# Second layer's down projection: seven block products (Strassen's scheme) for each pair of column slices, in seven of eight row slices

## The chip, the cores and the metric

The kernel runs on one core of one Trainium2 chip. The metric is the device time of one execution in microseconds (us), measured over several runs; the median counts. A profile of one execution stands beside it. Engines: TensorE (PE, with its weight loads PEld), VectorE (DVE), ScalarE (ACT), GpSimd (POOL), and SyncE (SP), which issues most of the transfers.

## The reference, cut to what matters

A trunk of two layers over 256 tokens of 2048 features, in float32; each layer is a token mixer and then a squared-ReLU MLP with 8192 hidden features:

```
def mlp(h, w_up, w_down):
    a = jax.nn.relu(h @ w_up)          # (256 x 2048) @ (2048 x 8192)
    return (a * a) @ w_down            # (256 x 8192) @ (8192 x 2048)

for i in range(2):
    ...
    h = rms_norm(x, mlp_norm[i])
    x = x + mlp(h, mlp_w_up[i], mlp_w_down[i])
return rms_norm(x, final_norm)
```

## The kernel before, in words

All weights stream from HBM once. The whole program is a list of steps; each step brings one weight tile `raw` of 1 MB (128 partitions, 2048 numbers each), and is worked off in two halves of 128x1024. `split` (L110) turns a half into two parts: `hi`, the number rounded to the TensorE's float32r format (ACT, L118), and `lo`, the rest `raw - hi` (L125, on DVE, or on POOL for steps listed in `pool_lo`). The activations are split in the same way. A product of float32 numbers is then three matmuls: hi x hi, lo x hi, hi x lo. `run_steps` (L159) keeps loads three steps ahead and splits three halves ahead of the half that PE consumes; `raw` has 3 buffers, `hi` and `lo` 4 halves each. Order and overlap on the engines are settled when the program is built, by a scheduler that places instructions by their dependences and priorities; the order on each engine is fixed after that.

`mlp` (from L685) cuts the 8192 hidden features into eight slices of 1024. `up(s)` computes slice s in four quarters q of 256 features, two steps each (kc = 0, 1); a half takes 8 matmuls of 512 columns (`mm_f`, L199) and 8 of 256 (L202), and at the end of a quarter `relu2` (L804) adds the two parts (DVE L808, one input in PSUM), applies max and the token scale (DVE L810), squares (ACT L812) and splits the result into `rT`. `down(s)` multiplies a slice's activations by 1024 rows of `w_down`, in four column slices n of 512 with two steps each. A half takes 12 matmuls of 512 columns (`mm_t`, L222 to L224): 2 row blocks of 128, 2 token blocks of 128, 3 each. After each n, DVE adds the accumulator to `x` (L820). The order is up(0), up(1), down(0), up(2), down(1), ..., up(7), down(6), down(7). The second layer's part begins at about 1270 us; the last slice, down(7), runs beside the final norm.

Of the kernel before, what the change touches and what calls it, by code (L numbers as in the profile page):

```python
# [2 lines left out]

# [15 lines left out]
P = 128  # L19
EPS = 1e-6  # L20
D = 2048
T = 256
# [11 lines left out]
URGENT = 300  # L34


class Trunk:
    def __init__(self, ctx, tc, a, out):
        self.tc, self.nc, self.a = tc, tc.nc, a
        self.out = out[0].rearrange("(b p) c -> p b c", p=P)  # L40
        self.DF = a["mlp_w_up"].shape[2]
        pool = lambda name, bufs, **k: ctx.enter_context(tc.tile_pool(name=name, bufs=bufs, **k))
        self.const = pool("const", 1)
        self.w = pool("w", 3)
        self.blk = pool("blk", 6)
# [4 lines left out]
        self.dram = pool("dram", 1, space=DRAM)  # L50
        self.steps = []
        self.pending = []
        self.bg = []
        self.rate = self.credit = 0
        self.raws, self.parts = {}, {}
# [8 lines left out]
        return self.blk.tile(shape, dt, tag="blk", name=name)  # L64

    def t4(self, shape, name="t4"):
        return self.tmp.tile(shape, F32, tag="t4", name=name)

    def t2(self, shape, name="t2"):
        return self.tmp.tile(shape, F32, tag="t2", name=name, bufs=3)  # L70
# [9 lines left out]
    def add(self, view, shape, consume, pre=None):  # L80
        self.steps.append((view, shape, consume, pre))

    def add_f(self, w2d, k0, c0, consume, pre=None):
        self.add(w2d[k0 * P:(k0 + 8) * P, c0:c0 + 256].rearrange("(k p) n -> p k n", p=P), [P, 8, 256], consume, pre)

# [6 lines left out]
            self.fetched = self.nc.sync.dma_start(out=out, in_=in_)  # L92

    def load(self, i, half=None):
        view, shape, _, _ = self.steps[i]
        for kind in self.before_load.pop(i, ()):
            self.table(*kind)
        if not half:
            self.raws[i] = self.w.tile(shape, F32, tag="raw", name="raw", bufs=3)
        raw = self.raws[i]  # L100
        nk = shape[1] // 2
        k = slice(0, shape[1]) if half is None else slice(half * nk, half * nk + nk)
        if len(shape) == 4:
            for j in range(shape[2]):
                self.fetch(raw[:, k, j, :], view[:, k, j, :])
        else:
            self.fetch(raw[:, k], view[:, k])
        self.loaded = i + 1

    def split(self, h, urgent=True):  # L110
        i, half = divmod(h, 2)
        raw = self.raws[i] if half == 0 else self.raws.pop(i)
        nk = raw.shape[1] // 2
        sl = raw[:, half * nk:(half + 1) * nk]
        hi = self.w.tile([P, nk] + list(raw.shape[2:]), F32R, tag="hi", name="hi", bufs=4)
        lo = self.w.tile([P, nk] + list(raw.shape[2:]), F32R, tag="lo", name="lo", bufs=4)
        with self.tc.high_priority(offset=URGENT if urgent else 0):
            self.nc.scalar.activation(hi, sl, AF.Copy)  # L118
            eng = self.nc.gpsimd if i in self.pool_lo else self.nc.vector
            if self.barrier is not None and h == 2 * self.barrier + 2:  # L120
                self.low_late = lambda: eng.tensor_tensor(out=lo, in0=sl, in1=hi.bitcast(F32), op=ALU.subtract)
                self.parts[h] = (hi, lo)
                return None
            with self.behind(self.lo_gate) if self.lo_gate is not None else nullcontext():
                ins = eng.tensor_tensor(out=lo, in0=sl, in1=hi.bitcast(F32), op=ALU.subtract)  # L125
# [33 lines left out]
    def run_steps(self):  # L159
        n = 2 * len(self.steps)  # L160
        ns = 0
        for h in range(n):
# [7 lines left out]
            while self.loaded < min(len(self.steps), i + 4):  # L170
# [4 lines left out]
            if half == 0 and pre is not None:  # L175
                pre()
            hi, lo = self.parts.pop(h)
# [233 lines left out]
    def conv_in(self):  # L411
# [28 lines left out]

    def gate(self, c, A):
        nc = self.nc
        b_in = self.vec("b_in")
        t = self.tmp.tile([P, T], F32, tag="ga", name="ga", bufs=2)
        with self.tc.high_priority(offset=URGENT):
            nc.vector.tensor_tensor(out=A, in0=A, in1=self.rstdB.broadcast_to([P, 2, T]), op=ALU.mult)
# [238 lines left out]
    def mlp(self, layer, last_slice, last_block, hooks=None):  # L685
        w_up, w_dn = self.a["mlp_w_up"][layer], self.a["mlp_w_down"][layer]
        nsl = self.DF // 1024
        rT = {}

        def up(s):  # L690
            for q in range(4):
                for kc in range(2):
                    def consume(hi, lo, half, q=q, kc=kc):
                        if kc == 0 and half == 0:
                            if q == 0:
                                rT[s] = self.blk_tile([P, 8, 2, T], F32R, name="rT")
                            rT["acc"] = self.acc2()
                        A = rT["acc"]
                        self.mm_f([A[:, 0], A[:, 1]], self.hT, hi, lo, kc * 8 + half * 4,
                                  kc == 0 and half == 0, kc == 1 and half == 1)  # L700
                        if kc == 1 and half == 1:
                            if s == 0 and q == 1 and layer == 0:
                                self.rate = 2.75
                            if s == 0 and q == 0:
                                self.after(1, lambda: self.relu2(A, rT[s], 2 * q))
                            else:
                                self.relu2(A, rT[s], 2 * q)
                    self.add_f(w_up, kc * 8, s * 1024 + q * 256, consume)

        def down(s):  # L710
            for n in range(NS):
                by_block = s == nsl - 1 and n == NS - 1
                for kc in range(2):
# [38 lines left out]
                    def consume_by_half(hi, lo, half, kc=kc):  # L752
# [3 lines left out]
                        for i, (b, c) in enumerate(((0, slice(0, 512)), (1, slice(0, 256)), (1, slice(256, 512)))):  # L756
                            with self.behind(self.mm_last):
                                self.mm_b(rT["acc"][i], lambda kk: rT[s][:, 2 * h + kk], hi, lo, b, c, h == 0, h == 3)
                            if h == 3:
# [5 lines left out]
                               consume if not by_block else consume_by_block if layer else consume_by_half,  # L765
                               (hooks or {}).get((nsl - 1 - s, n, kc)))

        up(0)
# [46 lines left out]

    def tt(self, out, a, b, op):
        return self.nc.vector.tensor_tensor(out=out, in0=a, in1=b, op=op)  # L820
# [315 lines left out]
    def ssm_slice(self, n):  # L1136
# [471 lines left out]
```

## Time and profile before

| | |
|---|---|
| median of 3 runs | 1987.26 us (1987.15 to 1990.01) |
| profiled execution | span 1985.8 us from first to last instruction; its own device time isn't listed apart |
| PE busy over the span | 1966.9 us (99%) |
| PEld | 1687.0 us (85%) |
| DVE | 1401.3 us (71%) |
| ACT | 952.4 us (48%) |
| POOL | 274.8 us (14%) |
| DMA | 428.49 MB, mean 216 GB/s |
| granted TensorE clock, mean | 0.999 |

Busy time is the time in which at least one instruction of an engine runs. A row of a group reads: line, engine, operation, written tile `<-` read tiles, shapes, count | busy time, mean ns of one | idle time of the engine just before, and what ended it. The profile's POOL work lies almost wholly in the first 250 us.

### The profile page before, as it was taken

How to read it: one execution, taken by the hardware profiler on the slowest of the kernel's cores; microseconds unless marked ns; L12 is line 12 of the kernel's file. 1: busy time of each engine (PE TensorE's matmuls, PEld its weight loads, DVE VectorE, ACT ScalarE, POOL GpSimd, SP SyncE). 2: the span in 40 equal slices, each digit the busy share in tenths (PEclk: the TensorE clock that was granted, in tenths of full speed). 3: DMA queues.
4: the chain of work that ended last, by engine and by line, in shares of the span. 5: the costliest groups of instructions: out<-in, count | busy, mean ns of one | idle time of the engine just before them, and what ended most of it. 6: DMA issues, size and time to landing. Idle time of an engine off the chain costs nothing.

```text
span 1985.8 us, 28885 instructions
## 1 busy us (share of the span) xinstructions
PE 1966.9 (99%) x11604; PEld 1687.0 (85%) x11604; DVE 1401.3 (71%) x1904; ACT 952.4 (48%) x1179; POOL 274.8 (14%) x252
## 2 busy tenths in 40 slices
PE   8999999999999999999999999999999999999998
PEld 8999788888888888888888788888888888888887
DVE  6899798888787777777558847565555565555655
ACT  6443655544444544444445445454444454444444
POOL 3998300000000221222010000000000000000000
PEclk9999999999999999999999999999999999999999
DMA  8767458667686877877898865665666656565653
GB/s 228 190 184 207 147 183 267 206 226 245 200 260 192 214 229 253 265 246 238 319 308 298 304 215 186 191 191 189 193 190 192 190 191 191 190 213 190 192 191 128
DMA packets 317030, 428.49 MB, mean 216 GB/s; under 512 B 9761, under 2 KB 211553, under 8 KB 313537
## 3 DMA queue, kind: packets, MB, share of 16 engines
q1 hardware_dynamic: 300976, 384.59, 61.6%
q0 software_dynamic: 12352, 37.49, 6.3%
q10 hardware_dynamic: 3568, 4.56, 0.8%
q8 instruction: 91, 1.49, 0.3%
q14 instruction: 43, 0.35, 0.1%
HBM read 400.08 MB, written 34.91 MB: 219 GB/s over the span
## 4 chain that ended last, share of the span: by engine, by line
PE 96%; DVE 2%; DMA 1%; issue 0%; SPq 0%; POOL 0%; ACT 0%; POOLq 0%; DVEq 0%; ACTq 0%
PE acc L199 24%; PE acc L222 15%; PE acc L223 15%; PE acc L224 15%; PE acc L202 12%; PE acc L213 3%; PE acc L212 3%; PE acc L211 3%; PE pk L484 1%; DMA Vt<-Vd 0%; SPq L92 0%; PE kp L1113 0%; PE xw L1254 0%; DMA raw<-in_conv_w_in_dram 0%; PE xt L254 0%
## 5 line engine op out<-in xcount | busy, mean ns | idle before, releaser
L118 ACT ACTIVATE hi<-raw 128x1024 fp32r<-128x1024 f32 x672 | 711.6, 1060 | 953.5 <-PE acc L224 510.2
L125 DVE TENSOR_TENSOR lo<-raw,hi 128x1024 fp32r<-128x1024 f32 x611 | 747.9, 1226 | 505.6 <-ACT hi L118 501.3
L199 PE MATMUL acc<-hT,hi 128*128 128x512 f32 x2048 | 514.4, 393 | 0.0
L199 PEld LDWEIGHTS acc<-hT,hi 128*128 128x128 f32 x2048 | 368.9, 189 | 68.0 <-issue 1.6
L222 PE MATMUL acc<-hi,rT 128*128 128x512 f32 x992 | 387.2, 391 | 0.0
L223 PE MATMUL acc<-lo,rT 128*128 128x512 f32 x992 | 386.4, 390 | 0.0
L224 PE MATMUL acc<-hi,rT 128*128 128x512 f32 x992 | 386.0, 389 | 0.0
L202 PEld LDWEIGHTS acc<-hT,lo 128*128 128x128 f32 x2048 | 279.6, 190 | 20.0
L202 PE MATMUL acc<-hT,lo 128*128 128x256 f32 x2048 | 286.3, 282 | 0.0
L222 PEld LDWEIGHTS acc<-hi,rT 128*128 128x128 f32 x992 | 186.3, 188 | 39.6 <-issue 1.6
L224 PEld LDWEIGHTS acc<-hi,rT 128*128 128x128 f32 x992 | 186.3, 188 | 39.1
L223 PEld LDWEIGHTS acc<-lo,rT 128*128 128x128 f32 x992 | 186.3, 188 | 38.0 <-issue 0.2
L125 POOL TENSOR_TENSOR lo<-raw,hi 128x1024 fp32r<-128x1024 f32 x60 | 143.1, 2402 | 31.3 <-ACT hi L118 24.8
L211 PE MATMUL acc<-hT,hi 128*128 128x256 f32 x512 | 146.1, 286 | 0.9 <-ACT hi L118 0.9
L212 PE MATMUL acc<-hT,hi 128*128 128x256 f32 x512 | 145.7, 286 | 0.3 <-DVE hT L259 0.3
L213 PE MATMUL acc<-hT,lo 128*128 128x256 f32 x512 | 145.5, 286 | 0.0
L829 DVE SCALAR_TENSOR_TENSOR cv<-vT,dw,cv 128x256 f32<-128x256 f32 x348 | 141.3, 486 | 2.2 <-ACT cv L527 1.7
L820 DVE TENSOR_TENSOR x<-x,acc 128x1024 f32<-128x1024 f32 (+1 forms) x72 | 83.6, 1161 | 27.6 <-PE acc L224 22.0
L211 PEld LDWEIGHTS acc<-hT,hi 128*128 128x128 f32 x512 | 98.9, 193 | 3.0 <-issue 1.6
L222 PE MATMUL acc<-hi,yT 128*128 128x512 f32 x256 | 101.1, 395 | 0.0
L212 PEld LDWEIGHTS acc<-hT,hi 128*128 128x128 f32 x512 | 98.8, 193 | 2.2 <-issue 1.6
L223 PE MATMUL acc<-lo,yT 128*128 128x512 f32 x256 | 99.9, 390 | 0.6 <-DVE lo L125 0.6
(285 smaller groups left out, 1722.9 us busy)
## 6 DMA issues: line engine op xcount, KB each, us to landing
raw<-in_mlp_w_up_dram SPq DMA_DIRECT2D x128, 1024.0 KB, 5.8
raw<-in_mlp_w_down_dram SPq DMA_DIRECT2D x128, 1024.0 KB, 5.2
raw<-in_ssm_w_glu_dram SPq DMA_DIRECT2D x32, 1024.0 KB, 5.5
raw<-in_conv_w_in_dram SPq DMA_DIRECT2D x60, 512.0 KB, 5.6
raw<-in_conv_w_out_dram SPq DMA_DIRECT2D x16, 1024.0 KB, 5.2
Vd<-bv POOLq DMA_DIRECT2D x16, 512.0 KB, 6.3
Md<-Kd POOLq DMA_DIRECT2D x32, 256.0 KB, 7.2
Wt<-Wd SPq DMA_DIRECT2D x8, 1024.0 KB, 10.1
```

The lines of the kernel that those rows point to most:

```text
L118: self.nc.scalar.activation(hi, sl, AF.Copy)
L125: ins = eng.tensor_tensor(out=lo, in0=sl, in1=hi.bitcast(F32), op=ALU.subtract)
L199: mm(accs[m], lhsT=hi[:, kk, cs[m]], rhs=xT(k0 + kk), start=first and kk == 0, stop=False)
L202: mm(accs[m][:, 0:T], lhsT=lo[:, kk, cs[m]], rhs=xT(k0 + kk)[:, 0, :], start=False, stop=last and kk == 3)
L211: mm(accs[m], lhsT=hi[:, kk, c], rhs=x[:, 0, :], start=first and kk == 0, stop=False)
L212: mm(accs[m], lhsT=hi[:, kk, c], rhs=x[:, 1, :], start=False, stop=False)
L213: mm(accs[m], lhsT=lo[:, kk, c], rhs=x[:, 0, :], start=False, stop=last and kk == 3)
L222: mm(acc[:, b, :], lhsT=ak[:, 0, t], rhs=hi[:, kk, :], start=first and kk == 0, stop=False)
L223: mm(acc[:, b, :], lhsT=ak[:, 0, t], rhs=lo[:, kk, :], start=False, stop=False)
L224: self.mm_last = mm(acc[:, b, :], lhsT=ak[:, 1, t], rhs=hi[:, kk, :], start=False, stop=last and kk == 1)
L820: return self.nc.vector.tensor_tensor(out=out, in0=a, in1=b, op=op)
L829: return self.nc.vector.scalar_tensor_tensor(out=out, in0=a, scalar=s, in1=b, op0=op0, op1=op1)
```

## The change

In the second layer (`layer == 1`), for row slices 0 to 6, `down` is replaced by `seven(s, 0)` and `seven(s, 2)`. Each handles two column slices. The 1024 x 1024 piece of `w_down` is read as four blocks of 512 x 512 by even and odd row blocks and left and right columns, K0 = B(0,0), K1 = B(0,1), K2 = B(1,0), K3 = B(1,1); the activations, two token blocks by the same even and odd rows, as four blocks of 128 tokens. Instead of eight block products there are seven, of sums of blocks. The weights' sums are formed in place by POOL (`K0-K1`, `K0-K3`, `K2-K0`, `K1-K3`, the second and third with K0 as changed so far); the activations' four sums by POOL in `relu2_forms`. A product's half is 6 matmuls of 512 columns. Four accumulator banks p, q, r, t are added to `x` by DVE.

The eight steps U0 to U7 of `up(s)` stand among the products E0 to E6 of the two column pairs of slice s-1:

`U0 U1 E0 E1 U2 E2 E3 U3 E4 E5 U4 E6 U5 E0 E1 U6 E2 U7 E3 E4 E5 E6`

E0 uses K0 as loaded, E1 `K0-K1`, E2 K2, E3 `K0-K3`, E4 K3, E5 `K2-K0`, E6 `K1-K3`. In the second layer's up, the steps of odd quarters (U2, U3, U6, U7) get their low part on POOL. In the whole kernel, raw tiles are now two halves in a pool of 6; K0 and K1 have a pool of their own (`wide`, 4 halves), in memory that the `t4` tiles used until then. The last slice, `down(7)`, and the first layer stay.

```
     def load(self, i, half=None):
...
+        if pre in ("sum", "held"):
+            return
+        key = None
+        if pre == "x":
+            key, shape = shape, [P, 4, 512]
+            if self.wide is None:
+                self.t4_guard.__exit__(None, None, None)
+                self.wide = self.ctx.enter_context(self.tc.tile_pool(name="wide", bufs=4))
         nk = shape[1] // 2
...
+            if key is not None and key[-1] in self.in_wide:
+                raw = self.wide.tile(size, F32, tag="wd", name="raw")
+            else:
+                raw = self.w.tile(size, F32, tag="raw", name="raw", bufs=6)
...
     def split(self, h, urgent=True):
...
+        elif pre == "sum":
+            key, a, b, op = key
+            sl = self.blocks[key + (half,)]
+            self.nc.gpsimd.tensor_tensor(out=sl, in0=self.blocks[a + (half,)], in1=self.blocks[b + (half,)], op=op)
...
+        def products(acc, s, i, hi, lo, half, first):
+            mm = partial(self.nc.tensor.matmul, acc, skip_group_check=True)
+            for jj in range(2):
+                F = rT[s][half][:, jj]
+                mm(lhsT=F[:, 0, i, :], rhs=hi[:, jj, :], start=first and half == jj == 0, stop=False)
+                mm(lhsT=F[:, 0, i, :], rhs=lo[:, jj, :], start=False, stop=False)
+                self.mm_last = mm(lhsT=F[:, 1, i, :], rhs=hi[:, jj, :], start=False, stop=half == jj == 1)
...
+            return [lambda: load(B(0, 0), key(0), part(A11, "p", True, take(c11, "p"))),
+                    lambda: (load(B(0, 1), key(1)),
+                             total(key(0), key(1), key(0), ALU.subtract, part(S1, "r", True, take(c22, "r")))),
+                    lambda: load(B(1, 0), key(2), part(A12, "q", True, take(c11, "q"))),
+                    lambda: (load(B(1, 1), key(3)),
+                             total(key(0), key(3), key(0), ALU.subtract, part(S2, "p", False, take(c12, "p")))),
+                    lambda: load_done(key(3), part(S4, "r", False, take(c12, "r"))),
+                    lambda: total(key(2), key(0), key(2), ALU.subtract, part(A22, "t", True, take(c21, "t", ALU.subtract))),
+                    lambda: total(key(1), key(3), key(1), ALU.subtract, part(S3, "p", False, both))]
...
+                    if layer and q % 2:
+                        self.pool_lo.add(len(self.steps))
                     self.add_f(w_up, kc * 8, s * 1024 + q * 256, consume)
...
         for s in range(1, nsl):
-            up(s)
-            down(s - 1)
+            if not formed(s - 1):
+                up(s)
+                down(s - 1)
+                continue
+            emit = seven(s - 1, 0) + seven(s - 1, 2)
+            at = [k * 7 // 4 * 9 // 10 for k in range(8)]
+            for i, e in enumerate(emit):
+                for k in range(8):
+                    if at[k] == i:
+                        up(s, k)
+                e()
...
+    def relu2_forms(self, acc, R):
...
+        nc.vector.tensor_tensor(out=t, in0=acc[:, :, 0:T], in1=t, op=ALU.add)
+        nc.vector.scalar_tensor_tensor(out=t, in0=t, scalar=0.0, in1=self.rstdB.broadcast_to([P, 2, T]),
+                                       op0=ALU.max, op1=ALU.mult)
...
+        pt = nc.gpsimd.tensor_tensor
+        pt(out=v[:, 0, :], in0=a21, in1=a22, op=ALU.add)
+        pt(out=v[:, 1, :], in0=v[:, 0, :], in1=a11, op=ALU.subtract)
+        pt(out=v[:, 2, :], in0=a11, in1=a21, op=ALU.subtract)
+        pt(out=v[:, 3, :], in0=a12, in1=v[:, 1, :], op=ALU.subtract)
+        self.hsplit(u[:, 1:4, :], R[:, 0, 0:3, :], R[:, 1, 0:3, :])
+        self.hsplit(v, R[:, 0, 3:7, :], R[:, 1, 3:7, :])
```

What stands on POOL before, from the state-space scan of the second layer to the end of the program (the second row belongs to the norm ahead of the second MLP, the third to the final norm):

```order
L1282 MEMSET m_10594 128x16
L286 TENSOR_TENSOR rstd_11806<-ssm_11804,mhalf_102 128x2
L1521 DMA gF_16796<-in_final_norm_dram 128x2048
L797 TENSOR_TENSOR rb_17017<-ssb_17015,mhalf_102 128x1
L1552 TENSOR_TENSOR rb_17058<-ssb_17059,mhalf_102 128x1
```

The same engine after, at the first column pair of one slice (halves of K0 are 16362 and 16364, of K1 16375 and 16377, of K2 16565 and 16567, of K3 16588 and 16590; 16510 and 16512 are U2, 16601 is U3's first half; `v` and `u` are the activations' sums):

```order
L149 TENSOR_TENSOR raw_16362<-raw_16375,raw_16362 128x1024
L149 TENSOR_TENSOR raw_16364<-raw_16377,raw_16364 128x1024
L149 TENSOR_TENSOR raw_16375<-raw_16588,raw_16375 128x1024
L149 TENSOR_TENSOR raw_16377<-raw_16590,raw_16377 128x1024
L149 TENSOR_TENSOR raw_16362<-raw_16588,raw_16362 128x1024
L162 TENSOR_TENSOR lo_16598<-raw_16510,hi_16597 128x1024
L947 TENSOR_TENSOR v_16552<-u_16551 128x128
L949 TENSOR_TENSOR v_16552<-u_16551 128x128
L149 TENSOR_TENSOR raw_16364<-raw_16590,raw_16364 128x1024
L162 TENSOR_TENSOR lo_16606<-raw_16512,hi_16605 128x1024
L149 TENSOR_TENSOR raw_16565<-raw_16362,raw_16565 128x1024
L948 TENSOR_TENSOR v_16552<-v_16552,u_16551 128x128
```

Where POOL had nothing between the norm and the final norm, it now has a chain of sums and low parts; the scheduler has put `K1-K3` ahead of the first `K0-K3`.

DVE before, in one down projection, two column slices' end (`x` gets the accumulator after every four low parts):

```order
L125 TENSOR_TENSOR lo_16499<-raw_16445,hi_16498 128x1024
L820 TENSOR_TENSOR x_80<-x_80,acc_16451 128x2x512
L125 TENSOR_TENSOR lo_16518<-raw_16445,hi_16517 128x1024
L125 TENSOR_TENSOR lo_16535<-raw_16480,hi_16534 128x1024
L125 TENSOR_TENSOR lo_16553<-raw_16480,hi_16552 128x1024
L125 TENSOR_TENSOR lo_16569<-raw_16515,hi_16568 128x1024
L820 TENSOR_TENSOR x_80<-x_80,acc_16521 128x2x512
```

DVE after, in the same column pair as POOL's rows, from K3's low parts (E4) on, with E5 (K2), U4 (16664, 16666) and E6's first half (16375); L955 is the add to `x`, L281 the low part of activations, L940 and L941 are in `relu2_forms`:

```order
L162 TENSOR_TENSOR lo_16715<-raw_16588,hi_16714 128x1024
L162 TENSOR_TENSOR lo_16726<-raw_16590,hi_16725 128x1024
L162 TENSOR_TENSOR lo_16747<-raw_16565,hi_16746 128x1024
L955 TENSOR_TENSOR x_83<-x_83,mr_16609 128x512
L162 TENSOR_TENSOR lo_16787<-raw_16567,hi_16786 128x1024
L281 TENSOR_TENSOR rT_16472<-v_16552,rT_16472 128x512
L162 TENSOR_TENSOR lo_16797<-raw_16664,hi_16796 128x1024
L162 TENSOR_TENSOR lo_16808<-raw_16666,hi_16807 128x1024
L162 TENSOR_TENSOR lo_16820<-raw_16375,hi_16819 128x1024
L940 TENSOR_TENSOR t_16766<-acc_16631,t_16766 128x512
L955 TENSOR_TENSOR x_83<-x_83,mt_16811 128x512
L941 SCALAR_TENSOR_TENSOR t_16766<-t_16766,bcs_12270 128x512
```

DVE's low parts of the down projection now stand for halves with 6 matmuls instead of 12, those of E5 and E6 wait for a sum of POOL, and the adds to `x` are smaller and more.

More of the change, by code (lines that the diff above doesn't have):

```diff
@@ L1 @@
 from contextlib import ExitStack, nullcontext
+from functools import partial
 import math
@@ L50, in __init__ @@
         self.dram = pool("dram", 1, space=DRAM)
+        self.ctx = ctx
+        self.t4_guard = tc.tile_pool(name="quad", bufs=4)
+        self.quad = self.t4_guard.__enter__()
+        self.wide = None
         self.steps = []
@@ L54, in __init__ @@
         self.rate = self.credit = 0
-        self.raws, self.parts = {}, {}
+        self.raws, self.parts, self.blocks = {}, {}, {}
+        self.in_wide = (0, 1)
         self.loaded = 0
@@ L81, in add, with add_block, add_sum @@
         self.steps.append((view, shape, consume, pre))
+    def add_block(self, view, key, consume=None):
+        self.steps.append((view, key, consume, "x"))
+    def add_sum(self, key, a, b, op, consume):
+        self.steps.append((None, (key, a, b, op), consume, "sum"))
     def add_f(self, w2d, k0, c0, consume, pre=None):
@@ L94, in load @@
     def load(self, i, half=None):
-        view, shape, _, _ = self.steps[i]
+        view, shape, _, pre = self.steps[i]
         for kind in self.before_load.pop(i, ()):
             self.table(*kind)
-        if not half:
-            self.raws[i] = self.w.tile(shape, F32, tag="raw", name="raw", bufs=3)
-        raw = self.raws[i]
-        nk = shape[1] // 2
[L102 to L107, printed above, removed]
@@ L108, in load @@
-        self.loaded = i + 1
+        self.loaded = i + 1
+        if pre in ("sum", "held"):
[6 more added lines that the diff above has]
+                self.wide = self.ctx.enter_context(self.tc.tile_pool(name="wide", bufs=4))
+        nk = shape[1] // 2
+        for hf in (0, 1) if half is None else (half,):
+            k = slice(hf * nk, hf * nk + nk)
+            size = [P, nk] + list(shape[2:])
+            if key is not None and key[-1] in self.in_wide:
+                raw = self.wide.tile(size, F32, tag="wd", name="raw")
+            else:
+                raw = self.w.tile(size, F32, tag="raw", name="raw", bufs=6)
+            if key is None:
+                self.raws[2 * i + hf] = raw
+            else:
+                self.blocks[key + (hf,)] = raw
+            if len(shape) == 4:
+                for j in range(shape[2]):
+                    self.fetch(raw[:, :, j, :], view[:, k, j, :])
+            else:
+                self.fetch(raw, view[:, k])
@@ L110, in split @@
     def split(self, h, urgent=True):
         i, half = divmod(h, 2)
[L112 to L116, printed above, removed]
+        _, key, consume, pre = self.steps[i]
+        if pre in ("x", "held"):
+            if consume is None:
+                return None
+            sl = self.blocks[key + (half,)]
+        elif pre == "sum":
+            key, a, b, op = key
+            sl = self.blocks[key + (half,)]
+            self.nc.gpsimd.tensor_tensor(out=sl, in0=self.blocks[a + (half,)], in1=self.blocks[b + (half,)], op=op)
+        else:
+            sl = self.raws.pop(h)
@@ L117, in split @@
+        hi = self.w.tile(list(sl.shape), F32R, tag="hi", name="hi", bufs=4)
+        lo = self.w.tile(list(sl.shape), F32R, tag="lo", name="lo", bufs=4)
         with self.tc.high_priority(offset=URGENT if urgent else 0):
@@ L161, in run_steps @@
         ns = 0
+        count = [0]
+        for step in self.steps:
+            count.append(count[-1] + (step[3] not in ("sum", "held")))
+        self.ahead = lambda i: count[i]
         for h in range(n):
@@ L169, in run_steps @@
                 pre, ns = None, self.presplit
-            while self.loaded < min(len(self.steps), i + 4):
+            while self.loaded < len(self.steps) and self.ahead(self.loaded) < self.ahead(i) + 4:
                 self.load(self.loaded)
@@ L174, in run_steps @@
                 ns += 1
-            if half == 0 and pre is not None:
+            if half == 0 and callable(pre):
                 pre()
+            if consume is None:
+                continue
             hi, lo = self.parts.pop(h)
@@ new lines, in seven, with part, consume, take @@
+        def seven(s, n):
+            v = w_dn[s * 1024:(s + 1) * 1024].rearrange("(k two p) c -> two p k c", two=2, p=P)
+            B = lambda r, c: v[r, :, :, (n + c) * 512:(n + c + 1) * 512]
+            x = self.x
+            c11, c12, c21, c22 = (x[:, b, (n + c) * 512:(n + c + 1) * 512] for b in range(2) for c in range(2))
+            c2 = x[:, 1, n * 512:(n + 2) * 512].rearrange("p (c j) -> p c j", c=2)
+            acc = {}
+            key = lambda i: (s, n, i)
+            def part(form, bank, first, done):
+                def consume(hi, lo, half):
+                    if first and half == 0:
+                        acc[bank] = self.bank([P, 512], name="m" + bank)
+                    products(acc[bank], s, form, hi, lo, half, first)
+                    if half == 1:
+                        with self.tc.high_priority(offset=URGENT):
+                            done()
+                return consume
+            def take(c, bank, op=ALU.add):
+                return lambda: self.tt(c, c, acc[bank], op)
+            def both():
+                self.tt(c2, c2, acc["p"].unsqueeze(1).broadcast_to([P, 2, 512]), ALU.add)
+            A11, A22, A12, S1, S2, S3, S4 = range(7)
+            load, total = self.add_block, self.add_sum
+            return [lambda: load(B(0, 0), key(0), part(A11, "p", True, take(c11, "p"))),
[7 more added lines that the diff above has]
+                    lambda: total(key(1), key(3), key(1), ALU.subtract, part(S3, "p", False, both))]
@@ L691, in up, with load_done @@
+        def load_done(key, consume):
+            self.steps.append((None, key, consume, "held"))
+        def up(s, only=None):
             for q in range(4):
                 for kc in range(2):
+                    if only is not None and only != 2 * q + kc:
+                        continue
                     def consume(hi, lo, half, q=q, kc=kc):
                         if kc == 0 and half == 0:
-                            if q == 0:
+                            if formed(s):
+                                if q % 2 == 0:
+                                    rT.setdefault(s, []).append(self.blk_tile([P, 2, 2, 7, P], F32R, name="rT"))
+                            elif q == 0:
@@ L696, in consume @@
                                 rT[s] = self.blk_tile([P, 8, 2, T], F32R, name="rT")
-                            rT["acc"] = self.acc2()
-                        A = rT["acc"]
+                            rT["uacc"] = self.acc2()
+                        A = rT["uacc"]
                         self.mm_f([A[:, 0], A[:, 1]], self.hT, hi, lo, kc * 8 + half * 4,
@@ L703, in consume @@
                                 self.rate = 2.75
+                            if formed(s):
+                                act = lambda: self.relu2_forms(A, rT[s][q // 2][:, q % 2])
+                            else:
+                                act = lambda: self.relu2(A, rT[s], 2 * q)
                             if s == 0 and q == 0:
-                                self.after(1, lambda: self.relu2(A, rT[s], 2 * q))
+                                self.after(1, act)
                             else:
-                                self.relu2(A, rT[s], 2 * q)
+                                act()
+                    if layer and q % 2:
+                        self.pool_lo.add(len(self.steps))
                     self.add_f(w_up, kc * 8, s * 1024 + q * 256, consume)
@@ L766, in down @@
                                (hooks or {}).get((nsl - 1 - s, n, kc)))
+        formed = lambda s: layer == 1 and s < nsl - 1
         up(0)
         for s in range(1, nsl):
-            up(s)
-            down(s - 1)
+            if not formed(s - 1):
+                up(s)
+                down(s - 1)
+                continue
+            emit = seven(s - 1, 0) + seven(s - 1, 2)
[5 more added lines that the diff above has]
+                e()
         down(nsl - 1)
@@ L813, in relu2 @@
         self.hsplit(u, rT[:, k:k + 2, 0, :], rT[:, k:k + 2, 1, :])
+    def relu2_forms(self, acc, R):
+        nc = self.nc
+        t = self.t2([P, 2, T], name="t")
+        u = self.t2([P, 4, P], name="u")
+        v = self.t2([P, 4, P], name="v")
+        nc.scalar.activation(t, acc[:, :, T:2 * T], AF.Copy)
+        nc.vector.tensor_tensor(out=t, in0=acc[:, :, 0:T], in1=t, op=ALU.add)
+        nc.vector.scalar_tensor_tensor(out=t, in0=t, scalar=0.0, in1=self.rstdB.broadcast_to([P, 2, T]),
+                                       op0=ALU.max, op1=ALU.mult)
+        nc.scalar.activation(u.rearrange("p (m b) t -> p m b t", m=2)[:, :, ::-1, :],
+                             t.rearrange("p m (b t) -> p m b t", b=2), AF.Square)
+        a21, a11, a22, a12 = (u[:, i, :] for i in range(4))
+        pt = nc.gpsimd.tensor_tensor
[5 more added lines that the diff above has]
+        self.hsplit(v, R[:, 0, 3:7, :], R[:, 1, 3:7, :])
     def tt(self, out, a, b, op):
```

3 lines of the change are left out of this document (1 added, 2 removed).

## The prediction

> **What bounds the kernel now.** I read the chain of work that ended last, then that chain through one slice of the second MLP, then the load of every engine in that slice.
>
> ```profile
> PE 96%; DVE 2%; DMA 1%; issue 0%; SPq 0%; POOL 0%; ACT 0%; POOLq 0%; DVEq 0%; ACTq 0%
> ...
> 1361.40 0.23 PE acc L222
> ...
> 1404.72 0.23 PE acc L224
> 1404.95 1.81 PE acc L199 x8
> ...
> 1316.71:1404.90 88.19, 88.19 (x449) 75.33 (x449) 52.73 (x55) 41.30 (x47) 0.00 (x0) 1.00 0.60 187
> ```
>
> The first line gives 96% of the span to TensorE. The next three are the chain in order of time: one slice's 192 down matmuls (L222 to L224) run from 1361.40 to 1404.95, without a gap, so each costs 43.55 / 192 = 0.227 us. The last line is the whole slice, up and down (columns: stretch, PE, PEld, DVE, ACT, POOL, granted clock, DMA share, GB/s): PE is busy for all 88.2 us at full clock, DVE for 52.7, ACT for 41.3, POOL not at all. TensorE is the bound here, and every microsecond of matmul saved counts as long as nobody else becomes late.
>
> **What the change removes.** A slice now needs 14 products of 2 halves x 6 matmuls = 168 instead of 192. That is 24 x 0.227 = 5.4 us in each of seven slices, 38 us in all; PE's need falls from 88.2 to 82.8 us a slice. If PE stayed the bound, the time would be 1987.3 - 38 = 1949 us.
>
> **What it adds, per slice**, with durations from these rows:
>
> ```profile
> L125 DVE TENSOR_TENSOR lo<-raw,hi 128x1024 fp32r<-128x1024 f32 x33 | 40.4, 1225 | 36.2 <-ACT hi L118 36.2
> L820 DVE TENSOR_TENSOR x<-x,acc 128x1024 f32<-128x1024 f32 x4 | 4.9, 1221 | 1.6 <-PE acc L224 1.6
> L238 DVE TENSOR_TENSOR rT<-u,rT 128x512 fp32r<-128x512 f32 x4 | 2.8, 692 | 0.0
> L808 DVE TENSOR_TENSOR t<-acc,t 128x512 f32<-128x512 f32 x4 | 2.7, 684 | 0.0
> ...
> L118 ACT ACTIVATE hi<-raw 128x1024 fp32r<-128x1024 f32 x252 | 267.3, 1061 | 367.2 <-PE acc L224 197.4 <-PE acc L199 167.0 <-issue 2.2
> ...
> L125 POOL TENSOR_TENSOR lo<-raw,hi 128x1024 fp32r<-128x1024 f32 x60 | 143.1, 2402 | 31.3 <-ACT hi L118 24.8 <-DVE rowsel L896 6.4
> L400 POOL TENSOR_TENSOR x<-x,bo 128x1024 f32<-128x1024 f32 x4 | 9.6, 2391 | 0.0
> L286 POOL TENSOR_TENSOR rstd<-ssm,mhalf 128x2 f32<-128x2 f32 x3 | 2.1, 705 | 245.5 <-DVE ssm L284 245.5
> ```
>
> - POOL, idle before, gets 16 block sums (8 sums of 2 halves) and 8 low parts (the up steps of odd q), all 128x1024 with two inputs: 24 x 2.40 = 57.6. Its 16 differences of 128x128 have no row. An eighth of 2.39 is 0.30 from below, the tiny `rstd` at 0.71 bounds them from above; I take 0.35, nearer the plain arithmetic: 5.6. POOL: **63.2**.
> - DVE, operations whose two inputs both lie in SBUF: 28 + 8 low parts x 1.23 = 44.3; per q one 512-wide `max/mult` and one 512-wide low part at 0.69 and one 384-wide at about 0.55, 4 x 1.93 = 7.7. Together **52.0**. Operations with one input in PSUM: 12 accumulator adds of 512 at 0.68, 2 of 1024 at 1.22, 4 `t` at 0.68: 13.3.
> - ACT: 44 high parts x 1.06 = 46.6, and some 10 for the activations: 57.
>
> By busy time each fits into 82.8 us: POOL 63, DVE 65, ACT 57. So the question is whether DVE and POOL can work at the same time. In this stage of before, POOL does nothing, so the answer has to come from elsewhere in the trace.
>
> **What POOL does to DVE.** Five times in the trace a two-SBUF-input operation of DVE runs into one on POOL. In order of time: first DVE's row, then POOL's.
>
> ```profile
> 105.17 1.68 DVE L569 TENSOR_TENSOR vT<-vT,shift 128x1024 f32<-128x1024 f32 x1
> 103.37 2.39 POOL L125 TENSOR_TENSOR lo<-raw,hi 128x1024 fp32r<-128x1024 f32 x1 [0.66 <-ACT hi L118]
> 178.91 2.41 DVE L569 TENSOR_TENSOR vT<-vT,shift 128x1024 f32<-128x1024 f32 x1
> 154.20 26.04 POOL L125 TENSOR_TENSOR lo<-raw,hi 128x1024 fp32r<-128x1024 f32 x11
> 210.63 1.74 DVE L569 TENSOR_TENSOR vT<-vT,shift 128x1024 f32<-128x1024 f32 x1
> 208.90 2.38 POOL L125 TENSOR_TENSOR lo<-raw,hi 128x1024 fp32r<-128x1024 f32 x1 [0.47 <-ACT hi L118]
> 1027.82 1.84 DVE L125 TENSOR_TENSOR lo<-raw,hi 128x1024 fp32r<-128x1024 f32 x1
> 1027.54 1.04 POOL L1165 COPY xr<-xJ 128x1024 f32<-128x1024 f32 x1 [4.07 <-DMA xJ<-xs]
> 1045.23 1.94 DVE L125 TENSOR_TENSOR lo<-raw,hi 128x1024 fp32r<-128x1024 f32 x1 [1.60 <-ACT hi L118]
> 1045.05 1.04 POOL L1165 COPY xr<-xJ 128x1024 f32<-128x1024 f32 x1 [8.41 <-DMA xJ<-xs]
> ```
>
> Undisturbed, such an operation takes 1.22. The overlaps with POOL are 0.59, 1.33, 0.65, 0.76 and 0.86, and DVE is longer by 0.46, 1.19, 0.52, 0.62 and 0.72: together 3.51 us longer for 4.19 of overlap, **84%**. POOL keeps its 2.40. So DVE all but stands still while POOL works, the low parts included. Not so where one input lies in PSUM:
>
> ```profile
> 100.00:150.00 50.00, 49.96 (x414) 48.19 (x414) 48.33 (x118) 22.48 (x28) 48.89 (x25) 1.00 0.66 178
> ...
> L446 DVE TENSOR_TENSOR acc<-acc,bcs 128x512 f32<-128x512 f32 x16 | 11.2, 698 | 10.0 <-PE acc L213 9.9
> ```
>
> There POOL and DVE are busy for 48.9 and 48.3 of 50 us, and an add from PSUM keeps its 0.70. In the changed slice only 13.3 us of DVE's work is of that kind.
>
> All five rows have POOL starting first; what happens when DVE starts first no row shows. The Trainium skill, "SBUF — State Buffer", section "SBUF: two separate sides", has the pair of ports that the two engines share as an exclusive lock, taken by whichever starts first for its whole instruction, by a DVE operation with two SBUF inputs too; by that rule POOL would then wait. The rows above agree for the direction they show; the rule speaks against this change.
>
> **The sum.** Work that excludes each other adds up: 63.2 + 52.0 = **115.2 us a slice**, the 13.3 from PSUM lie beside POOL, and PE's 82.8, ACT's 57 and the loads lie beside all of it. Against 88.2 this is 27.0 more, seven times 189. The last of the seven periods computes slice 7's up, whose activations have no differences on POOL: -5.6. Together +183. The first slice's up alone holds on POOL 8 x 2.40 + 5.6 = 24.8, on DVE 8 x 1.23 + 7.7 = 17.5, together 42 of its 16 x 2.79 = 44.7 us of PE: nothing. I take the same 84% as a full stop, without credit for the 16%, because the order leaves idle gaps on both engines: around U0, U1 and around U4, U5 (two up steps with DVE low parts, 2 x 1.23 against 5.6 us of PE each) POOL has no sum ready, since a sum overwrites a block whose low part must be done first, and only four halves are split ahead. I put these gaps at up to 9 us a slice. Ends: with the 16% credited, 115.2 - 0.16 x 57.6 = 106.0 a slice, +119, and 0.30 instead of 0.35, -6: 2100. With 9 us of gaps 124, +245: 2232; with 0.71 for the differences, 6 more in six slices: 2267.
>
> What else moves costs nothing by these rows. Raw tiles are loaded by halves in the whole kernel, so SP issues twice as many transfers:
>
> ```profile
> raw<-in_mlp_w_up_dram SPq DMA_DIRECT2D x128, 1024.0 KB, 5.8
> ...
> raw<-in_conv_w_in_dram SPq DMA_DIRECT2D x60, 512.0 KB, 5.6
> ```
>
> A half lands no later than a whole, and in the earlier stages PE covers it; uncovered it would be one landing, 5.8 us. K0 of the next group waits for POOL's last sum with the old K0, then 5.6 for its transfer and 2.3 for its split; four steps (E5, U4, E6, U5, 17 us of PE) lie between. U4's transfer waits for K3 on SP's queue, with K0 and K1 of the next group behind it. These waits belong to the 9 us of gaps. The seven small adds go to DVE at high priority, ahead of low parts, with 10.6 - 4.9 = 6 us more a slice, which lie beside POOL's work. The four `t4` tiles move to a pool that is closed before the wide blocks are opened, once, under 45 us of up: nothing. 1985.8 is the profiled span; I add 1.5 around it, so the sum stands against the median 1987.3: 1987.3 + 183 = **2170 us**.
>
> **Rivals.**
> - *PE stays the bound* (faster, 1949): POOL's sums run ahead into times when DVE waits, and DVE's low parts slip between them. For it: each engine's own load is under 82.8, and DVE idled 36 of 89 us for ACT's `hi`. Against it: the slice would need 115.2 - 82.8 = 32 of POOL's 63 us to run beside DVE's two-input work, half of it, and the five rows allow 16%. It decides at 88.2, where 27 of the 63 (43%) must overlap; below that the kernel is slower than before.
> - *Only the later one stops* (about 2070): a DVE operation that has started goes on beside POOL. At most 24 x 1.2 = 29 a slice is then shared, 86 a slice and the old time; with half of it, 101 a slice, +84. No row excludes it. By the lock of the skill's page it gets no share.
> - *PE loses its clock as well* (2240 and more): its waits get long enough.
>
> ```profile
> 0.00:20.00 20.00, 14.19 (x88) 13.43 (x88) 13.64 (x36) 13.39 (x27) 0.80 (x7) 1.00 0.95 275
> ...
> 1976.80:1986.00 9.20, 1.30 (x11) 1.09 (x10) 3.19 (x10) 2.46 (x4) 0.56 (x1) 0.83 0.62 228
> ```
>
> With PE busy for 71% of the first 20 us the clock stays at 1.00; at 14% it falls to 0.83. Here PE would be busy for 82.8 of 115, 72%. If half of the matmuls ran at half clock, PE's need were 124 a slice, +245. The Trainium skill, "TensorE: Matmul & The Clock Gate", section "Part 1: The HAM clock gate", halves the clock after an idle window of about 3.4 us; by that rule one POOL operation of 2.4 us in PE's way is harmless and two in a row are not; the 0.83 above agrees in direction.
> - *The change doesn't do what it says* (1987 or so): excluded by the order of instructions, which has the 168 matmuls and 16 sums.
>
> **Chances.** DVE and POOL in turn, 2100 to 2250: 0.78. Only the later one stops, 1991 to 2100: 0.07. Clock or load loops on top, over 2250: 0.06. PE the bound, or nearly, under 1983: 0.07; within 0.2% (about what a measurement of this kernel can tell from no change): 0.02. The first case alone leaves out a little over 2 in 10; I take the range down to 2085 into the second. Faster has the 0.07 of the fourth case, slower the 0.91 of the first three.
>
> **What would show it.** In a slice of the changed kernel: a period of about 115 us; POOL's and DVE's busy times together over 115, because a blocked operation counts as busy, so `lo` on DVE (or POOL's 2.40) reads well above 1.23; PE's idle ended by DVE `lo`, some by POOL; accumulator adds from PSUM unchanged at 0.68; clock near 1.00. A mean `lo` of 1.3 with POOL at 2.4 would prove me wrong, as would PE's idle ended by transfers.

## The result, and the profile after

| | before | after |
|---|---|---|
| median | 1987.2 us (4 runs) | 2169.4 us (4 runs, 2165.1 to 2179.0) |
| ratio to before, 95% interval | | 1.092 [1.090, 1.095] |
| span of the profiled execution | 1985.8 us | 2167.9 us |

The kernel became slower by 182 us. Two rows of the page after, engines first and the chain that ended last second:

```profile
PE 2007.4 (93%) x11436; PEld 1685.3 (78%) x11436; DVE 1658.9 (77%) x1994; ACT 1043.1 (48%) x1291; POOL 878.0 (41%) x540
...
PE 71%; DVE 11%; issue 7%; POOL 6%; DMA 2%; ACT 2%; SPq 0%; POOLq 0%; DVEq 0%; ACTq 0%
```

There are 168 matmuls fewer, and yet of the chain, which was 96% PE, only 71% are left on PE; the rest lies mostly on DVE, on POOL and in `issue`, time for which the profile shows no cause. A slice is measured by DVE's last add of a column pair, of which each slice has two; the rows that begin and end five whole slices:

```profile
1434.82 1.22 DVE L955 TENSOR_TENSOR x<-x,mp 128x1024 f32<-128x1024 f32 x1
...
2004.31 1.22 DVE L955 TENSOR_TENSOR x<-x,mp 128x1024 f32<-128x1024 f32 x1
```

That is 569.5 / 5 = 113.9 us a slice, against 88.2 before. The groups of DVE and of POOL in the stretch from 1330 to 2100 us show where it goes (mean ns of one behind the busy time):

```profile
L162 DVE TENSOR_TENSOR lo<-raw,hi 128x1024 fp32r<-128x1024 f32 x240 | 421.4, 1782 | 73.4 <-ACT hi L155 71.2 <-PE acc L245 1.3 <-PE mr L738 0.2
L941 DVE SCALAR_TENSOR_TENSOR t<-t,bcs 128x512 f32<-128x512 f32 x24 | 41.5, 1729 | 0.6
L281 DVE TENSOR_TENSOR rT<-v,rT 128x512 fp32r<-128x512 f32 x25 | 29.8, 1193 | 23.8 <-ACT rT L280 23.8
L955 DVE TENSOR_TENSOR x<-x,mr 128x512 f32<-128x512 f32 x27 | 18.4, 680 | 8.3 <-PE mr L739 7.9
L940 DVE TENSOR_TENSOR t<-acc,t 128x512 f32<-128x512 f32 x24 | 16.4, 683 | 17.3 <-ACT t L939 17.3
...
L149 POOL TENSOR_TENSOR raw<-raw 128x1024 f32<-128x1024 f32 x109 | 310.4, 2868 | 134.5 <-DVE lo L162 131.7 <-DMA raw<-in_mlp_w_down_dram 1.6 <-issue 1.2
L162 POOL TENSOR_TENSOR lo<-raw,hi 128x1024 fp32r<-128x1024 f32 x56 | 158.0, 2824 | 17.5 <-ACT hi L155 16.4 <-issue 1.1
```

Everything on DVE that reads two tiles from SBUF has become longer: the low part reads 1.78 instead of 1.23, the max/mult of 512 columns 1.73 where 0.69 is normal. What reads one operand from PSUM is unchanged (0.68). POOL's operations are longer too, 2.82 to 2.87 instead of 2.40. What PE waited for, from 1270 us on (total, times, longest):

```profile
PE mr L738 <- DVE lo L162: 40.8, 24, 4.2
PE mq L738 <- DVE lo L162: 32.9, 11, 5.6
PE mp L738 <- DVE lo L162: 31.5, 13, 4.0
PE mp L737 <- ACT hi L155: 12.2, 12, 1.8
PE mr L737 <- ACT hi L155: 12.1, 16, 1.5
```

PE stood mostly for low parts, then for high parts. ACT makes the high parts, some of them from POOL's sums, and what it waited for most were these sums (73.3 us from 1320 to 1900). No wait of PE is put down to a transfer. A stretch of some 16 us shows the collision in both directions. First DVE, then POOL:

```profile
1600.00 2.35 DVE L162 TENSOR_TENSOR lo<-raw,hi 128x1024 fp32r<-128x1024 f32 x2
1602.27 0.55 DVE L281 TENSOR_TENSOR rT<-u,rT 128x384 fp32r<-128x384 f32 x1
1613.85 2.18 DVE L941 SCALAR_TENSOR_TENSOR t<-t,bcs 128x512 f32<-128x512 f32 x1
...
1601.28 1.86 POOL L947 TENSOR_TENSOR v<-u 128x128 f32<-128x128 f32 x1 [8.08 <-ACT u L943]
1603.10 0.46 POOL L949 TENSOR_TENSOR v<-u 128x128 f32<-128x128 f32 x1
1612.02 3.45 POOL L149 TENSOR_TENSOR raw<-raw 128x1024 f32<-128x1024 f32 x1 [1.16 <-DVE lo L162]
```

POOL's difference at 1601.28 arrives while DVE works through two low parts and a part of `rT`, to 1602.82: it takes 1.86, and its neighbour, with nobody ahead of it, 0.46. At 1613.85 it is the other way round: POOL's sum runs to 1615.47, and DVE's 0.69 us operation takes 2.18. The Trainium skill, "SBUF — State Buffer", section "SBUF: two separate sides", calls this an exclusive lock that goes to whichever starts first; the 1.86 against 0.46 is the direction that the trace of before didn't show, and it agrees. One detail does not follow from that rule: this operation waited also for the part of `rT`, which started after it. After 1300 us, 178 operations of POOL met a running two-input operation of DVE, and six of them waited for more than that one.

The stop is complete but for a small fixed piece. An operation that had to wait ends a fixed time after the one that it waited for, and this time is its undisturbed duration less some 0.14 us: DVE's 1.22, 0.69 and 0.55 become 1.08, 0.55 and 0.41, POOL's 0.46 becomes 0.32 and its 2.40 becomes 2.20 to 2.28, in almost every such case of this trace. The prediction's five overlaps show the same: overlap and lengthening differ by 0.13 or 0.14 us each time, however long the overlap.

### The profile page after: what moved, and what is told of

Read it like the earlier page. It is cut to its first block, busy times and chain, and to the rows that moved or that the text cites. A ratio compares the mean times of both kernels' runs of the same rounds, so it can differ in the third digit from the quotient of the medians.

```text
span 2167.9 us, 30186 instructions
## 1 busy us (share of the span) xinstructions
PE 2007.4 (93%) x11436; PEld 1685.3 (78%) x11436; DVE 1658.9 (77%) x1994; ACT 1043.1 (48%) x1291; POOL 878.0 (41%) x540
## 4 chain that ended last, share of the span: by engine, by line
PE 71%; DVE 11%; issue 7%; POOL 6%; DMA 2%; ACT 2%; SPq 0%; POOLq 0%; DVEq 0%; ACTq 0%
PE acc L242 16%; PE acc L265 9%; PE acc L266 9%; PE acc L267 9%; PE acc L245 9%; DVE lo L162 7%; POOL raw L149 3%; PE acc L254 3%; PE acc L256 3%; PE acc L255 3%; ACT hi L155 2%; POOL lo L162 1%; DMA raw<-in_mlp_w_down_dram 1%; PE mr L738 1%; DVE t L941 1%
## 5 line engine op out<-in xcount | busy, mean ns | idle before, releaser
L155 ACT ACTIVATE hi<-raw 128x1024 fp32r<-128x1024 f32 x756 | 792.2, 1058 | 945.4 <-PE acc L267 332.0
L162 DVE TENSOR_TENSOR lo<-raw,hi 128x1024 fp32r<-128x1024 f32 x631 | 904.3, 1444 | 332.7 <-ACT hi L155 328.3
L242 PEld LDWEIGHTS acc<-hT,hi 128*128 128x128 f32 x2048 | 375.3, 191 | 76.0 <-ACT hi L155 5.3
L162 POOL TENSOR_TENSOR lo<-raw,hi 128x1024 fp32r<-128x1024 f32 x124 | 321.8, 2603 | 263.2 <-ACT hi L155 252.0
L149 POOL TENSOR_TENSOR raw<-raw 128x1024 f32<-128x1024 f32 x112 | 319.6, 2873 | 134.5 <-DVE lo L162 131.7
L265 PE MATMUL acc<-hi,rT 128*128 128x512 f32 x544 | 212.9, 392 | 0.0
L266 PE MATMUL acc<-lo,rT 128*128 128x512 f32 x544 | 212.1, 390 | 0.0
L267 PE MATMUL acc<-hi,rT 128*128 128x512 f32 x544 | 211.7, 389 | 0.0
L265 PEld LDWEIGHTS acc<-hi,rT 128*128 128x128 f32 x544 | 102.1, 188 | 22.6 <-issue 1.6
L267 PEld LDWEIGHTS acc<-hi,rT 128*128 128x128 f32 x544 | 102.1, 188 | 21.5
L266 PEld LDWEIGHTS acc<-lo,rT 128*128 128x128 f32 x544 | 102.2, 188 | 20.7 <-issue 0.2
L254 PEld LDWEIGHTS acc<-hT,hi 128*128 128x128 f32 x512 | 98.5, 192 | 3.7 <-issue 2.1
L738 PE MATMUL mp<-lo,rT 128*128 128x512 f32 x168 | 71.4, 425 | 31.5 <-DVE lo L162 31.5
```

The source lines that it names most:

```text
L149: self.nc.gpsimd.tensor_tensor(out=sl, in0=self.blocks[a + (half,)], in1=self.blocks[b + (half,)], op=op)
L242: mm(accs[m], lhsT=hi[:, kk, cs[m]], rhs=xT(k0 + kk), start=first and kk == 0, stop=False)
L254: mm(accs[m], lhsT=hi[:, kk, c], rhs=x[:, 0, :], start=first and kk == 0, stop=False)
L265: mm(acc[:, b, :], lhsT=ak[:, 0, t], rhs=hi[:, kk, :], start=first and kk == 0, stop=False)
L266: mm(acc[:, b, :], lhsT=ak[:, 0, t], rhs=lo[:, kk, :], start=False, stop=False)
L267: self.mm_last = mm(acc[:, b, :], lhsT=ak[:, 1, t], rhs=hi[:, kk, :], start=False, stop=last and kk == 1)
```

## Experiments

Three theories. A: DVE operations with two SBUF inputs and POOL's reads exclude each other, so their times add up. B: POOL is merely slow, and stands in the chain of sum, split and product. C: PE lost clock because it waited (its clock in the changed stage was 0.90). All ratios are to the kernel before, with their 95% intervals.

| run | median, us | ratio |
|---|---|---|
| pool_reads | 2126.4 | 1.070 [1.068, 1.072] |
| pool_fills | 1997.7 | 1.005 [1.003, 1.007] |
| sums_dve | 2054.6 | 1.034 [1.032, 1.036] |
| all_dve | 2002.0 | 1.008 [1.006, 1.009] |
| no_sums | 1951.8 | 0.982 [0.980, 0.984] |
| warm | 2181.8 | 1.098 [1.096, 1.100] |
| half | 1975.4 | 0.994 [0.992, 0.996] |
| pool_lo_alone | 1987.7 | 1.000 [0.999, 1.001] |
| mix | 1981.0 | 0.997 [0.995, 0.998] |

**pool_reads**: the kernel before, with useless reads on POOL.

```
         self.hsplit(u, rT[:, k:k + 2, 0, :], rT[:, k:k + 2, 1, :])
+            both = rT[:, k:k + 2].bitcast(F32)
+            for _ in range(8):
+                nc.gpsimd.tensor_tensor(out=self.spare..., in0=both, in1=both, op=ALU.add)
```

> The kernel before, and in the second MLP, at the end of each up quarter, POOL adds the quarter's fresh activations (128x1024, two inputs in SBUF) to themselves 8 times into a spare tile that nobody reads: 32 x 2.39 = 76.5 us of POOL a slice, on which no engine waits. DVE's two-SBUF-input work there is 32 x 1.23 + 8 x 0.42 + 4 x 0.69 = 45.4. If POOL and DVE exclude each other (theory A), a slice takes 110 to 122 us instead of 88.2: 2150 to 2260 us in all, and DVE's low parts read well above 1.23. If the change was slower only because POOL's slow operations stand in the chain of sum, split, product (theory B), or because PE lost its clock (theory C), nothing changes: 1987.

DVE's low parts and POOL's adds from 1320 to 1900 us:

```profile
L126 DVE TENSOR_TENSOR lo<-raw,hi 128x1024 fp32r<-128x1024 f32 x173 | 409.2, 2402 | 27.8 <-ACT hi L119 27.7
...
L821 POOL TENSOR_TENSOR spare<-rT 128x1024 f32<-128x1024 f32 x191 | 483.1, 2529 | 99.7 <-DVE rT L239 85.1
```

139 us slower, though no wait of PE, ACT or DVE in this stage is put down to POOL: B and C can't give that. The low part needs 2.40 instead of 1.23. The size is below what A was said to give, 2150: 139 / 8 slices = 17 us a slice instead of 22 to 34. That is because the expectation priced these adds too high. One that starts first, and the low part that meets it:

```profile
1778.23 1.90 POOL L821 TENSOR_TENSOR spare<-rT 128x1024 f32<-128x1024 f32 x1 [20.14 <-DVE rT L239]
...
1778.93 2.28 DVE L126 TENSOR_TENSOR lo<-raw,hi 128x1024 fp32r<-128x1024 f32 x1 [0.84 <-ACT hi L119]
```

The add of a tile to itself takes 1.90, not the 2.39 of an operation with two different inputs, and the low part ends 1.08 after it, as in the changed kernel. With 1.90 the sum is 32 x 1.90 + 45.4 = 106 us a slice; five whole slices took 104 each.

**pool_fills**: fills in place of the reads.

```
-            for _ in range(8):
-                nc.gpsimd.tensor_tensor(out=self.spare..., in0=both, in1=both, op=ALU.add)
+            nc.gpsimd.tensor_copy(out=self.spare[:, 0:2], in_=rT[:, k + 1, 1, 0:2].bitcast(F32))
+            for _ in range(20):
+                nc.gpsimd.memset(self.spare, 1.0)
```

> The same, with 20 fills of the spare tile (128x1024, about 1 us each by the slope of the fills in the trace of before) in place of the 8 adds, after a tiny copy that paces them: POOL as busy, some 75 us a slice, but without reading SBUF. Theory A, if the reads are what collides: 1987, low parts at 1.23. If any work on POOL stops DVE: 2130 or more. B and C: 1987.

The first two rows are the same groups as above, the third POOL's last entries in order of time:

```profile
L126 DVE TENSOR_TENSOR lo<-raw,hi 128x1024 fp32r<-128x1024 f32 x211 | 258.4, 1225 | 228.0 <-ACT hi L119 228.0
L821 POOL MEMSET spare<- 128x1024 f32 x559 | 533.9, 955 | 32.2
...
1980.31 11.35 POOL L821 MEMSET spare<- 128x1024 f32 x11
```

POOL is even busier, 534 of 580 us, and the low part keeps its 1.225. PE was busy without a gap in these 580 us. The 10 us more lie at the end: eleven fills left over, which run on POOL when TensorE is done, and for which the end of the program waits. So it isn't POOL's work as such that stops DVE, but what these adds do and fills don't: read SBUF. The kind of instruction differs too; but POOL's copies at 1027 and 1045 us in the prediction's rows, which read one tile, stopped DVE as the sums do.

**sums_dve**: the block sums on DVE.

```
-            self.nc.gpsimd.tensor_tensor(out=sl, in0=self.blocks[a + (half,)], ...
+            self.nc.vector.tensor_tensor(out=sl, in0=self.blocks[a + (half,)], ...
```

> The changed kernel with the 16 block sums a slice on DVE. Theory A: POOL 8 x 2.40 + 16 x 0.46 = 26.6, DVE with two SBUF inputs 52.0 + 16 x 1.23 = 71.7, together 98.3 a slice against 113.8 measured: 2169 - 7 x 15.5 = 2061. Theory B, without exclusion: DVE's own load is the bound, 71.7 + 13.3 = 85.0, just above PE's 82.8: 1965 to 1990. Theory C: as PE waits less, somewhere between.

2055: A's sum held to 7 us, B's 1965 to 1990 did not come. Work moved from POOL (busy for 428 of the 580 us from 1320 to 1900) onto DVE, which was the busier one (448), made the kernel 115 us faster.

**all_dve**: nothing left on POOL.

```
-                    if layer and q % 2:
-                        self.pool_lo.add(len(self.steps))
...
-        pt = nc.gpsimd.tensor_tensor
+        pt = nc.vector.tensor_tensor
```

> The changed kernel with all of POOL's part on DVE: sums, low parts of the odd quarters, activations' differences. DVE alone: 60 x 1.14 to 1.23, 7.7, 16 x 0.25, 13.3 = 93 to 99 a slice. Theory A: 2020 to 2065, and no slower than with only the sums moved, though an engine is given up. Theory B: slower than with only the sums moved, because DVE's load grows from 85 to 96. Low parts at 1.23 in both.

The groups of DVE, and the row of busy times by engine (PE, PEld, DVE, ACT, POOL, clock), both from 1320 to 1900:

```profile
L162 DVE TENSOR_TENSOR lo<-raw,hi 128x1024 fp32r<-128x1024 f32 x280 | 336.2, 1220 | 0.0
L149 DVE TENSOR_TENSOR raw<-raw 128x1024 f32<-128x1024 f32 x104 | 125.3, 1220 | 6.4 <-DMA raw<-in_mlp_w_down_dram 6.4
...
1320.00:1900.00 580.00, 548.69 (x2714) 448.98 (x2713) 573.54 (x673) 342.31 (x383) 0.62 (x1) 1.00 0.56 182
```

2002, another 53 us less and 18 below the range. DVE is now the bound, 573.5 of 580 us; low parts and sums are back at 1.22, and the clock at 1.00. The six whole slices take 90.9 us on average and not 93: DVE's 104 operations of a slice add up to 98.2 us, but back to back each overlaps the next by 0.08 at its end, which leaves 89.7.

**no_sums**: the sums left out.

```
-            self.nc.gpsimd.tensor_tensor(out=sl, in0=self.blocks[a + (half,)], ...
```

> The changed kernel without the 16 block sums a slice: E1, E3, E5, E6 multiply K0, K0, K2, K1 as loaded. Theory A: POOL 26.6, DVE with two SBUF inputs 52.0, together 78.6, below PE's 82.8: PE is the bound again, 1950 to 1980. Theory B: the same. It sizes the share of the sums: about 190 to 220 of the loss.

1952: with POOL's remaining 26.6 and DVE's 52.0, together 78.6, below PE's 82.8, the saving on PE comes out, 36 of the 38 us. This run alone doesn't tell A from B, which expected the same.

**warm**: more matmuls where PE waited.

```
                 mm(lhsT=F[:, 0, i, :], rhs=hi[:, jj, :], start=first and half == jj == 0, stop=False)
+                for _ in range(3 if jj == 0 else 0):
+                    mm(lhsT=F[:, 0, i, :], rhs=self.zero, start=False, stop=False)
```

> The changed kernel with three more matmuls of 512 columns in each product half, against a tile of zeros, between the first high part's matmul and the low part's: 28 x 3 x 0.227 = 19 us more of PE a slice, in the place where it waited for DVE. Theory C (the clock is what is lost): granted clock back to 0.98 or more and the time down by 40 us or more. Theory A: PE has the room (82.8 + 19 = 102 below 113.8), so the time stays within 1% of 2169 although the clock rises.

Busy times and clock from 1320 to 1900, the changed kernel first:

```profile
1320.00:1900.00 580.00, 480.63 (x2169) 386.41 (x2168) 448.33 (x335) 270.86 (x306) 427.60 (x206) 0.90 0.45 146
```

```profile
1320.00:1900.00 580.00, 538.08 (x2550) 437.70 (x2549) 466.52 (x332) 263.18 (x302) 423.50 (x203) 0.98 0.44 144
```

The clock rose from 0.90 to 0.98, and the time went up by 12 us instead of down by 40. C falls as the cause of the loss: the lower clock cost nothing that can be seen. A small cost could hide behind the added matmuls, some 19 us of PE a slice; that is not separated here.

**pool_lo_alone**: that one line of the change in the kernel before.

```
+                    if layer and q % 2:
+                        self.pool_lo.add(len(self.steps))
                     self.add_f(w_up, kc * 8, s * 1024 + q * 256, consume)
```

> The kernel before with one part of the change: in the second MLP the low parts of the up steps of odd quarters on POOL. POOL 8 x 2.40 = 19.2, DVE with two SBUF inputs 24 x 1.23 + 6.2 = 35.7, together 54.9, far below PE's 88.2. Theory A: 1987 within 0.3%, though single low parts read up to 3.6. Theory B: the same or a few us more.

1987.7, as before. DVE's max/mult of 256 columns reads 0.70 instead of 0.42 there, so the collision is present, but 54.9 us of such work stay under PE's 88.2.

**half**: Strassen's scheme for one of the two column pairs, all on DVE.

```
-            emit = seven(s - 1, 0) + seven(s - 1, 2)
+            emit = seven(s - 1, 0) + plain(s - 1, 2) + plain(s - 1, 3)
```

(`plain` is the old down product from the eight activation forms; all_dve's edits are in it, and the up steps stand at other places.)

> Seven products for the first pair of column slices only, the other pair by plain products from the same activations (an eighth form, A21, is kept), and all sums, low parts and differences on DVE, none on POOL. PE needs 88.2 - 2.7 = 85.5 a slice; DVE 38 low parts and 8 sums at 1.14 to 1.23, 4.0, 5.5, 2.8, 2.7, 7.7 = 75 to 80. Theory A: nothing collides, PE stays the bound: 1968 to 1985, unless DVE's bursts of sums make PE wait (then up to 2005). Theory B: the same.

1975.4: below both kernels. Against the kernel before it is a small gain, 0.6%, but clear of its interval: 12 of the 19 us that PE saves. Of the rest, PE waited 6.4 us in all, once a slice for 0.9 us, for an up step's high part:

```profile
PE acc L242 <- ACT hi L155: 6.4, 7, 0.9
```

**mix**: full and half slices in turn.

```
+            if s % 2:
+                emit = seven(s - 1, 0) + plain(s - 1, 2) + plain(s - 1, 3)
...
+            else:
+                emit = seven(s - 1, 0) + seven(s - 1, 2)
```

> As half, but in slices 1, 3 and 5 (counted from 0) both pairs of column slices by seven products, in 0, 2, 4 and 6 only the first; nothing on POOL. Theory A with DVE's loads as measured: a full slice took 1987.9 to 2002.0, so 88.2 + 2.0 = 90.2 us with DVE as the bound; a half one 88.2 - 12.3 / 7 = 86.4. If each slice keeps its own bound: 1987.7 + 3 x 2.0 - 4 x 1.8 = 1987. If DVE can work off in the half slices what it owes from the full ones (DVE 90.2 + 78 against PE 82.8 + 85.5 in a pair): about 1970. Only four halves are split ahead, so the first is likelier: 1980 to 1988, slower than half.

1981.0, between the two forecasts, nearer the one in which each slice keeps its own bound; not better than half.

## Why the prediction was right

- *What is removed*: right. no_sums has PE as the bound and gains 36 of the 38 us.
- *DVE and POOL exclude each other*: right, and it is the cause. pool_reads makes the loss without any of the change, pool_fills takes the collision out and leaves POOL busy, sums_dve takes part of it out of the changed kernel, all_dve the whole. Five overlaps in earlier stages of the trace were enough to foresee it. (Two of them lie after 1000 us: of the 275 us that POOL is busy before, 175 lie in the first 250, and not almost all.)
- *The sum*: 115.2 us a slice were forecast and 113.9 measured, 2170 against 2169.4, but that it came so close is luck, because terms cancelled. The 128x128 differences were undersized: 0.46 undisturbed, not 0.35, which makes 117.0. Dropping the credit of 16% (9.2 us) against the gaps was a choice; with the intervals of DVE's two-input operations and POOL's laid over each other from 1434.82 to 2004.31, neither runs for 32.0 of 569.5 us, 6.4 a slice. The other 107.5 us of a slice held the 117.0, so 9.5 were hidden. Both terms were real, and of similar size. The hidden part is no share of the overlap, as the prediction took it: it is for the most part the 0.14 us at each change from one engine to the other, 51 in a slice; the ends of operations that follow each other on one engine add 1.6. And the last slice was to be 5.6 us shorter; it took 113.3 (2004.31 to 2117.56).
- *Only the later one stops*: refuted as a saving. Both engines wait, each for the other.
- *PE loses its clock*: it did, 0.90 in the stage, where "near 1.00" was written; the price that the rival put on it did not come, as warm shows. The inference from the first 20 us (71% busy, clock 1.00) failed: the busy share was 83% here and the clock lower. The Trainium skill, "TensorE: Matmul & The Clock Gate", section "Part 1: The HAM clock gate", lets the clock fall after an idle window of some 3.4 us. Waits up to 5.6 us with 0.90 agree in direction; but in warm no wait of PE from 1280 to 1940 is longer than 1.9 us, and the clock of the stage is still 0.98, so here that rule is not the whole account.
- *What hides the rest*: transfers end no wait of PE directly. How much of the 6.4 us of gaps comes from buffers that were freed late was not tried.

## What to carry to other kernels

Idle time on GpSimd is not free capacity: before elementwise work that reads SBUF goes there, count it together with everything on VectorE that reads two tiles from SBUF, and compare the sum, not each engine, with the bound. A 128x1024 operation moved from VectorE to GpSimd took 2.40 us of that common time here instead of 1.22, so it pays only beside operations that read from PSUM or while the sum stays below the bound. A saving on the bound engine is worth what the second engine leaves over: here, with all of it on VectorE, half of the scheme gained 0.6%, and the whole of it did not gain.

## What was not expected of the hardware

That the stop costs each blocked operation its whole wait less some 0.14 us, on DVE and on POOL alike, and not a share of the overlap. That POOL adds a 128x1024 tile to itself in 1.90 us, and two different tiles in 2.40. And that fills on POOL, 92% of the time, did not lengthen DVE's two-input operations at all (1.225).
